# Routing ahead of the token split in a mixture-of-experts block: order of VectorE's work, layout of the tokens, and order of the first gather

## The chip, the cores and the metric

The kernel runs on one core of a Trainium2 chip. The metric is device time of one execution in microseconds (us), the median of several runs.

## The reference

One block of a diffusion transformer for 256 tokens of 1024 channels: modulation, input projections, four mixers (attention, a long convolution, two recurrences), a gated merge, and then a hierarchical mixture of experts. The change lies in the last:

```python
def _hier_moe(h, w_grp, b_grp, w_rt, b_rt, w1, w3, w2):
    t = h.reshape(-1, D_MODEL)
    gp = jax.nn.softmax((t @ w_grp + b_grp).astype(jnp.float32), axis=-1)
    g_val, g_idx = lax.top_k(gp, 1)                    # one of 4 groups
    el = (t @ w_rt + b_rt).astype(jnp.float32).reshape(-1, N_GROUPS, EXPERTS_PER_GROUP)
    el = jnp.take_along_axis(el, g_idx[:, :, None], axis=1)[:, 0]
    e_val, e_idx = lax.top_k(jax.nn.softmax(el, axis=-1), TOP_K_INNER)   # 2 of its 4 experts
    wts = g_val * e_val / jnp.sum(e_val, -1, keepdims=True)
    e_glob = g_idx * EXPERTS_PER_GROUP + e_idx
    combine = jnp.sum(jax.nn.one_hot(e_glob, N_EXPERTS, dtype=jnp.float32) * wts[..., None], axis=1)
    out = jnp.zeros_like(t)
    for e in range(N_EXPERTS):
        y = (jax.nn.silu(t @ w1[e]) * (t @ w3[e])) @ w2[e]
        out = out + combine[:, e:e + 1] * y
```

The block's result is `x + g2x * _hier_moe(_modulate(x, sh2x, sc2x), ...)`. Each expert has w1 and w3 of 1024x512 and w2 of 512x1024, all in float32.

## The kernel before, in words

Tokens lie on the 128 partitions in two halves (`a` = 0, 1). After the merge the kernel has `x2` (the tokens), `rx` (one over their root mean square) and the router's scores `lg`. From there:

- Choice. `rk` counts for each score how many of its four are larger; `og` is the chosen group, `sel` a 0/1 table of the two chosen experts, `oh` the first and second choice apart. `gm`, `ge`, `gv`, `so`, `w` are the weights (two exponentials, `ge` and `w`, run on ScalarE).
- Counting. Five small TensorE products of `sel` with ones and a triangle (`cntw`) give the tokens of each expert (`pn`, copied to `cntt`) and each token's place among its expert's (`pr`, copied to `pos`). `pm` is that place for the two static experts.
- Ranking. Experts 0 and 1 are static: 128 rows each. The other 14 are ranked by their count (`key`, `big`, `rank`, `roh`) and get rows in seven packed groups. `eidi` is the list of ranked experts; SyncE reads it into registers to address the weights of all later groups.
- Token split. `h2h` is the token times `rx` in the short float format of TensorE, `h2l` what rounding left. Half 0 of `h2l` is computed on VectorE, half 1 on GpSimd out of `sct`. ScalarE makes `h2h` and `sct`. Both tiles are laid out in 8 blocks of 128 channels, block j holding each eighth channel.
- Gather. `gather(gp)` brings the rows of two groups into `gT` by products with a 0/1 matrix `Dh` (256 columns): for each of the 8 blocks, two token halves, `h2h` and `h2l`, 32 products into PSUM tiles `mb`. The stationary side is a 128x128 block of `h2h` or `h2l`. ScalarE evicts the even blocks, VectorE the odd ones (`g<-mb,c`). There are five gathers.
- Experts. `expert_up` multiplies the gathered rows with w1 and w3 (PSUM tiles `hb`), `hidden` and `expert_down` follow, and a scatter by matrix product.

Weights come in 512 KB pieces on SyncE's queue into a ring of places (`wh`, `wwA`, `wB`, `wC`, `wD`, two of `g`); a place is free when TensorE has used its piece. The first 24 pieces belong to the static experts; later ones need `eidi`.

A scheduler sets the order of the instructions on each engine by what they depend on and by the order of the code; `after(x, y)` tells it to put x behind y, with no wait of its own. All operations go through one recording helper, so nearly every instruction of the profile has its line, L279; tile names tell them apart. L1550 is the read of `eidi` into a register. In a name such as `mb<-Dh,h2h` the tile after the comma is the stationary one.

Of the kernel before, what the change touches and what calls it, by code (L numbers as in the profile page):

```python
# [18 lines left out]
D = 1024  # L19
# [6 lines left out]
NSTAT = 2  # L26
# [260 lines left out]
def body(ctx, tc, I, out, dbg=None, upto=None):  # L287
    nc = tc.nc

    def after(ins, other):  # L290
        tc.add_manual_dep(ins.ins, other.ins.name, mybir.DependencyInfo(
            mybir.DependencyClass.NoSync, mybir.DependencyReason.SCHED_ONLY), reason="loads in order")
# [7 lines left out]
    def tap(name, ap):  # L300
        if name in dbg:
            nc.sync.dma_start(dbg[name], ap)
# [40 lines left out]
    def act(o, i, f=AF.Copy, **k):  # L343
        A.activation(out=o, in_=i, func=f, **k)

    def stt(o, a, s, b, op0=mul, op1=add, eng=V):
        return eng.scalar_tensor_tensor(out=o, in0=a, scalar=s, in1=b, op0=op0, op1=op1)

    def ts(o, a, s1, s2=None, op0=mul, op1=add, eng=V):
        if s2 is None:  # L350
            eng.tensor_scalar(out=o, in0=a, scalar1=s1, scalar2=None, op0=op0)
        else:
            eng.tensor_scalar(out=o, in0=a, scalar1=s1, scalar2=s2, op0=op0, op1=op1)

    def tt(o, a, b, op=mul, eng=V):
        eng.tensor_tensor(out=o, in0=a, in1=b, op=op)

    def cpy(o, i):
        return V.tensor_copy(out=o, in_=i)

    def red(o, i, op=add):
        return V.tensor_reduce(out=o, in_=i, axis=AX.X, op=op)
# [962 lines left out]
    def cl(name):  # L1325
        o, n = _CN[name]
        return late[:, o:o + n]
# [47 lines left out]
    def sm(name, shape, bufs=1, dt=F32):  # L1375
        return small(name, shape, bufs, p2, dt)
# [21 lines left out]
    ts(og, rk_[:, :, 0], 0.0, None, ALU.is_equal)  # L1398
    og4 = og.unsqueeze(3).to_broadcast([P, 2, 4, 4])
    sel = sm("sel", [2, 16], 1, F32R)  # L1400
    stt(sel.rearrange("p a (g e) -> p a g e", g=4), rk_[:, :, 1:5], 2.0, og4, ALU.is_lt, mul)

    pr, pn = mm(), mm()[:, :16]
    mmul(pn, cnt_w[:, 0], sel[:, 0], True, False)
# [1 line left out]
    mmul(pr[:, 0:16], cnt_w[:, 1], sel[:, 0])  # L1406
    mmul(pr[:, 16:32], cnt_w[:, 0], sel[:, 0], True, False)
    mmul(pr[:, 16:32], cnt_w[:, 1], sel[:, 1], False, True)

    nd = len(RANK)  # L1410
    key = sm("key", [nd])
    stt(key, pn[:, NSTAT:], 16.0, cl("rev"), mul, add)
    big3 = sm("big3", [nd, nd])
    rank = sm("rank", [nd])
    tt(big3, key.unsqueeze(1).to_broadcast([P, nd, nd]), key.unsqueeze(2).to_broadcast([P, nd, nd]), ALU.is_gt)
    ranked = red(rank, big3)
    roh = sm("roh", [nd, nd])
    tt(roh, rank.unsqueeze(1).to_broadcast([P, nd, nd]), cl("iota")[:, :nd].unsqueeze(2).to_broadcast([P, nd, nd]), ALU.is_equal)
    eidf, eidi = sm("eidf", [nd]), sm("eidi", [nd], 1, I32)
    big3 = sm("big3", [nd, nd])  # L1420
    tt(big3, roh, cl("eid").unsqueeze(1).to_broadcast([P, nd, nd]))
    red(eidf, big3)
    cpy(eidi, eidf)
    tap("eid", eidf)

    pos = sm("pos", [2, 16])
    after(cpy(pos, pr[:, 0:32].rearrange("p (a e) -> p a e", a=2)), ranked)
    pm = sm("pm", [2, NSTAT])
    stt(pm, pos[:, :, :NSTAT], 1.0, sel[:, :, :NSTAT].bitcast(F32), add, mul)

# [8 lines left out]
        return mb_("mb")  # L1439


    h2h, h2l = (slots.tile(p2, [P, 2, 8, 128], F32R, n, n, 1) for n in ("h2h", "h2l"))
    for a in range(2):
        xv = x2[:, a].rearrange("p (c j) -> p j c", j=8)
        act(h2h[:, a], xv, AF.Copy, scale=rx[:, a:a + 1])
        if a:
            for hf in range(2):
                t = slots.tile(p2, [P, 512], F32, "sct", "sct", 2)
                act(t, x2[:, a, hf * 512:hf * 512 + 512], AF.Copy, scale=rx[:, a:a + 1])
                hs = slice(hf * 64, hf * 64 + 64)  # L1450
                tt(h2l[:, a, :, hs], t.rearrange("p (c j) -> p j c", j=8), h2h[:, a, :, hs].bitcast(F32), sub, eng=G)
        else:
            stt(h2l[:, a], xv, rx[:, a:a + 1], h2h[:, a].bitcast(F32), mul, sub)


    cntt = sm("cntt", [16])
    cpy(cntt, pn)
    sb_, sc_ = sm("sb", [16]), sm("sc", [16])
    for dst, nm in ((sb_, "base"), (sc_, "cap")):
        cpy(dst[:, :NSTAT], cl("s" + nm))  # L1460
# [2 lines left out]
        red(dst[:, NSTAT:], big3)  # L1463
    oh = sm("oh", [2, 2, 16])
    for c in range(2):
        stt(oh[:, c].rearrange("p a (g e) -> p a g e", g=4), rk_[:, :, 1:5], float(c), og4, ALU.is_equal, mul)
    gm, ge, gv = sm("gm", [2, 1]), sm("ge", [2, 4]), sm("gv", [2, 1])
    red(gm, lg[:, :, 0:4], ALU.max)
    tt(ge, lg[:, :, 0:4], gm.to_broadcast([P, 2, 4]), sub)
    act(ge, ge, AF.Exp)  # L1470
    red(gv, ge)
# [88 lines left out]

    def gather(gp):

        Dh = slots.tile(p2, [P, 2, 256], F32R, "Dh", "Dh", 1)
        if gp == 0:
            for a in range(2):
                for e in range(2):
                    es = slice(e * 128, e * 128 + 128)
                    ts(Dh[:, a, es], cl("iota1"), pm[:, a, e:e + 1], None, ALU.is_equal)
            for a in range(2):
                for e in range(2):  # L1570
                    es = slice(e * 128, e * 128 + 128)
                    ts(Dw[:, a, es], cl("iota1"), pm[:, a, e:e + 1], we[:, a, e:e + 1], ALU.is_equal, mul)
        else:
            for a in range(2):
                ts(Dt[:, a], cl("iota"), sg[:, 0, a, gp:gp + 1], None, ALU.is_equal)
                stt(Dh[:, a], cl("iota"), sg[:, 1, a, gp:gp + 1], Dt[:, a], ALU.is_equal, add)
            for a in range(2):
                ts(Dt[:, a], Dt[:, a], w12[:, 0, a:a + 1])
                ts(Dw[:, a], cl("iota"), sg[:, 1, a, gp:gp + 1], w12[:, 1, a:a + 1], ALU.is_equal, mul)
                tt(Dw[:, a], Dw[:, a], Dt[:, a], add, eng=G)  # L1580
        for j2 in range(4):
            pg = mb()
            for jj in range(2):
                o = pg[:, jj * 256:jj * 256 + 256]
                j = 2 * j2 + jj
                for a in range(2):
                    mmul(o, h2h[:, a, j], Dh[:, a], a == 0, False)
                    mmul(o, h2l[:, a, j], Dh[:, a], False, a == 1)
                if jj:
                    ts(gT[:, j], o, c2[:, 1, j:j + 1], c2[:, 0, j:j + 1])  # L1590
                else:
                    act(gT[:, j], o, AF.Identity, scale=c2[:, 1, j:j + 1], bias=c2[:, 0, j:j + 1])

# [132 lines left out]
    with tc.If(over > 0):  # L1726
        slots.last.clear()
        cwl = sm("cwl", [2, 16])
        tt(cwl, we, lt_)
        for a in range(2):  # L1730
            hs_ = slots.tile(p2, [P, 8, 128], F32, "yeh", "yeh", 1)
            tt(hs_, h2h[:, a].bitcast(F32), h2l[:, a].bitcast(F32), add)
            for j4 in range(2):
                pt = mb()
                for jj in range(4):
                    j = 4 * j4 + jj
                    tr(pt[:, jj * 128:jj * 128 + 128], hs_[:, j])
                    act(gT[:, j, a * 128:a * 128 + 128], pt[:, jj * 128:jj * 128 + 128], AF.Identity,
                        scale=c2[:, 1, j:j + 1], bias=c2[:, 0, j:j + 1])
        for e in range(NE):  # L1740
            w13 = [[wload(name, e, q) for q in range(4)] for name in ("w1", "w3")]
            w2_ = [wload("w2", e, q) for q in range(4)]
            for a in range(2):
                as_ = slice(a * 128, a * 128 + 128)
                ph = []
                for ws in w13:
                    p = hb()
                    ph.append(p)
                    for j in range(8):
                        mmul(p, gT[:, j, as_], ws[j // 2][:, (j % 2) * 512:(j % 2) * 512 + 512], j == 0, j == 7)  # L1750
                a_ = slots.tile(p2, [P, 512], F32, "act", "act", 1)
                act(a_, ph[0], AF.Silu)
                tt(a_, a_, ph[1])
                pt = mb()
                for j in range(4):
                    tr(pt[:, j * 128:j * 128 + 128], a_[:, j::4])
                aT = slots.tile(p2, [P, 4, 128], F32, "aT", "aT", 1)
                act(aT.rearrange("p j s -> p (j s)"), pt)
                for hf in range(2):
                    hs = slice(hf * 512, hf * 512 + 512)  # L1760
                    po = mb()
                    for j in range(4):
                        mmul(po, aT[:, j], w2_[j][:, hs], j == 0, j == 3)
                    t = slots.tile(p2, [P, 512], F32, "sct", "sct", 2)
                    stt(t, po, cwl[:, a, e:e + 1], gg[0][:, 1, hs], mul, mul)
                    tt(x2[:, a, hs], x2[:, a, hs], t, add)
            places.extend(w13[0] + w13[1] + w2_)
        for a in range(2):
            SP.dma_start(ov[:, a], x2[:, a])
# [24 lines left out]
```

## Time and profile before

| | us |
|---|---|
| median of three runs | 779.45 |
| lowest and highest run | 777.98, 786.99 |
| profiled execution | 787.27 |
| its span in the trace | 785.5 |
| granted TensorE clock, mean share of full speed | 0.955 |
| TensorE busy | 720.7 (92%) |
| VectorE busy | 473.6 (60%) |
| ScalarE busy | 283.8 (36%) |
| GpSimd busy | 176.2 (22%) |

The span is the time from the first instruction to the last in the profiled execution; its own time is 1.8 us longer. The expert part takes the last third, from about 505 us. Starts in the rows below are us from the start of the span.

### The profile page before, as it was taken

The numbers are of one execution on the slowest core, as the hardware profiler recorded it, in microseconds if no ns is written. First come the engines' busy times: TensorE is split into PE (matmuls) and PEld (weight loads), VectorE is DVE, ScalarE is ACT, GpSimd is POOL, SyncE is SP. The second block draws the span as 40 slices with busy tenths as digits, with TensorE's granted clock in tenths as the row PEclk, the third lists the DMA queues.
The fourth block names the chain that finished last, engine by engine and source line by source line (L and its number), as shares of the span: only waits on it lengthen the run. The fifth ranks groups of instructions, "written<-read, shape, count | busy, mean of one in ns | idle before, by whom it ended". The sixth has DMA issues, their size and how long they took to land.

```text
span 785.5 us, 13522 instructions
## 1 busy us (share of the span) xinstructions
PE 720.7 (92%) x5155; PEld 503.6 (64%) x5155; DVE 473.6 (60%) x950; ACT 283.8 (36%) x530; POOL 176.2 (22%) x151
## 2 busy tenths in 40 slices
PE   3989998998889999999789998969999999999997
PEld 1658987887768667677689997754543434443334
DVE  5655467999993775899985377780422511432415
ACT  4333453533524676745346443440201102101111
POOL 0232232325421121122546474310000000000000
PEclk9979996999987999999989999969999999999999
DMA  8743220223332124668657688659799999999931
GB/s 321 246 182 108 86 76 28 55 82 109 111 105 55 29 81 162 195 213 288 202 207 269 220 298 308 240 168 410 274 376 409 408 408 409 409 409 410 388 99 57
DMA packets 53897, 174.97 MB, mean 223 GB/s; under 512 B 5442, under 2 KB 12482, under 8 KB 53826
## 3 DMA queue, kind: packets, MB, share of 16 engines
q1 hardware_dynamic: 50896, 168.79, 59.9%
q10 hardware_dynamic: 2930, 5.25, 2.0%
q8 instruction: 42, 0.69, 0.3%
q14 instruction: 29, 0.24, 0.1%
HBM read 172.97 MB, written 1.05 MB: 222 GB/s over the span
## 4 chain that ended last, share of the span: by engine, by line
PE 72%; DVE 20%; issue 3%; ACT 2%; POOL 1%; DMA 1%; SPq 0%; DVEq 0%; ACTq 0%; POOLq 0%
PE hb L279 26%; PE pj L279 18%; PE mm L279 14%; PE mo L279 9%; PE mb L279 7%; DVE wlo L279 3%; DVE TT L279 2%; DVE acc L279 2%; DVE tq L279 2%; DVE xt L279 1%; DVE L L279 1%; DVE gg L279 1%; DVE sin L279 1%; DVE hrc L279 1%; DMA hfp<-in_hfp_dram 1%
## 5 line engine op out<-in xcount | busy, mean ns | idle before, releaser
L279 PE MATMUL pj<-h,whi 128*128 128x256 f32 x1072 | 207.8, 293 | 4.7 <-DVE ylr L279 2.2
L279 PEld LDWEIGHTS pj<-h,whi 128*128 128x128 f32 x1072 | 172.6, 197 | 15.9 <-issue 9.3
L279 PE MATMUL pj<-h,wlo 128*128 128x256 f32 x536 | 158.8, 297 | 11.1 <-DVE wlo L279 10.5
L279 POOL TENSOR_TENSOR wlo<-raw,whi 128x512 fp32r<-128x512 f32 x64 | 90.0, 1405 | 196.2 <-ACT whi L279 176.4
L279 ACT ACTIVATE whi<-raw 128x512 fp32r<-128x512 f32 x130 | 81.1, 628 | 128.5 <-PE pj L279 105.9
L279 PEld LDWEIGHTS pj<-h,wlo 128*128 128x128 f32 x536 | 105.7, 197 | 15.9 <-DVE wlo L279 12.5
L279 DVE TENSOR_TENSOR wlo<-raw,whi 128x512 fp32r<-128x512 f32 x66 | 56.8, 861 | 23.3 <-ACT whi L279 23.0
L279 DVE TENSOR_TENSOR act<-act,hb 128x512 f32<-128x512 f32 x9 | 6.2, 688 | 96.7 <-PE hb L279 83.7
L279 PE MATMUL hb<-wwA,g 128*128 128x512 f32 (+2 forms) x200 | 59.8, 596 | 0.0
L279 POOL TENSOR_TENSOR gg<-gg 128x256 f32<-128x256 f32 x8 | 5.8, 741 | 183.0 <-DVE gg L279 183.0
L279 ACT ACTIVATE yeh<-sct,cw 128x512 fp32r<-128x512 f32 (+2 forms) x21 | 13.7, 661 | 76.1 <-DVE sct L279 75.6
L279 PEld LDWEIGHTS hb<-wwA,g 128*128 128x128 f32 (+2 forms) x200 | 20.8, 147 | 29.4 <-issue 27.2
L279 DVE TENSOR_TENSOR sct<-hb,gg 128x512 f32<-128x512 f32 (+2 forms) x21 | 12.8, 615 | 42.2 <-PE hb L279 42.2
L279 DVE SCALAR_TENSOR_TENSOR gg<-adaw,sT,gg 128x512 f32<-128x512 f32 x32 | 29.1, 931 | 2.4 <-ACT gg L279 2.3
L279 DVE TENSOR_TENSOR x<-mb,x 128x512 f32<-128x512 f32 (+2 forms) x42 | 23.7, 608 | 11.0 <-PE mb L279 11.0
L279 ACT ACTIVATE aT<-mb 128x512 f32<-128x512 f32 x9 | 5.4, 598 | 64.4 <-PE hb L279 33.4
L279 PE MATMUL mb<-Dh,h2h 128*128 128x256 f32 x80 | 24.1, 329 | 4.4 <-DVE eidi L279 3.7
L279 DVE SCALAR_TENSOR_TENSOR acc<-adaw,sT,acc 128x512 f32<-128x512 f32 x32 | 26.9, 874 | 0.0
L279 PE MATMUL hb<-wB,aT 128*32 128x512 f32 (+3 forms) x116 | 25.8, 508 | 0.0
L279 PE MATMUL hb<-wwA,aT 128*64 128x512 f32 (+2 forms) x96 | 24.1, 595 | 0.0
L279 PEld LDWEIGHTS mb<-Dh,h2h 128*128 128x128 f32 x80 | 16.8, 210 | 11.4 <-ACT g L279 4.1
L279 PE MATMUL hb<-wC,g 128*32 128x512 f32 (+2 forms) x88 | 23.4, 599 | 0.0
(482 smaller groups left out, 1455.0 us busy)
## 6 DMA issues: line engine op xcount, KB each, us to landing
wwA<-in_w_dram SPq DMA_DIRECT2D x72, 512.0 KB, 10.1
raw<-in_w_in_dram SPq DMA_DIRECT2D x57, 512.0 KB, 3.7
adaw<-in_ada_dram SPq DMA_DIRECT2D x48, 512.0 KB, 4.8
wB<-in_w_dram SPq DMA_DIRECT2D x35, 512.0 KB, 10.1
wC<-in_w_dram SPq DMA_DIRECT2D x24, 512.0 KB, 10.1
wh<-in_w_dram SPq DMA_DIRECT2D x22, 512.0 KB, 10.1
wD<-in_w_dram SPq DMA_DIRECT2D x17, 512.0 KB, 10.1
wb<-in_w_dram SPq DMA_DIRECT2D x10, 512.0 KB, 10.1
```

The source lines that it names most:

```text
L279: r = f(*a, **k)
```

## The change

The choice, the counts, the places and the first `Dh` (now `Dh0`) come ahead of VectorE's half of `h2l`, and this comes ahead of the ranking. First and second choice apart (`oh`), the largest group score (`gm`) and what follows from them come after the ranking. `key` reads the copy `cntt` and not PSUM. `h2h` and `h2l` keep the channels in their order, so that ScalarE, VectorE and GpSimd write and read them contiguously, and the products of all gathers read the stationary block with a stride of 8 elements (`j::8`). The first gather runs its 16 products with `h2h` before its 16 with `h2l`, into four PSUM tiles; VectorE's evictions of it stand behind the ranking.

```diff
-    stt(sel.rearrange("p a (g e) -> p a g e", g=4), rk_[:, :, 1:5], 2.0, og4, ALU.is_lt, mul)
+    selected = stt(sel.rearrange("p a (g e) -> p a g e", g=4), rk_[:, :, 1:5], 2.0, og4, ALU.is_lt, mul)
...
+    pos = sm("pos", [2, 16])
+    cpy(pos, pr[:, 0:32].rearrange("p (a e) -> p a e", a=2))
+    cntt = sm("cntt", [16])
+    cpy(cntt, pn)
+    pm = sm("pm", [2, NSTAT])
+    stt(pm, pos[:, :, :NSTAT], 1.0, sel[:, :, :NSTAT].bitcast(F32), add, mul)
...
+    h2h, h2l = (slots.tile(p2, [P, 2, D], F32R, n, n, 1) for n in ("h2h", "h2l"))
+    for a in range(2):
+        act(h2h[:, a], x2[:, a], AF.Copy, scale=rx[:, a:a + 1])
+    for hf in range(2):
+        t = slots.tile(p2, [P, 512], F32, "sct", "sct", 2)
+        hs = slice(hf * 512, hf * 512 + 512)
+        act(t, x2[:, 1, hs], AF.Copy, scale=rx[:, 1:2])
+        after(G.tensor_tensor(out=h2l[:, 1, hs], in0=t, in1=h2h[:, 1, hs].bitcast(F32), op=sub), selected)
+
+    Dh0 = slots.tile(p2, [P, 2, 256], F32R, "Dh", "Dh", 1)
+    for a in range(2):
+        for e in range(2):
+            es = slice(e * 128, e * 128 + 128)
+            last_dh = V.tensor_scalar(out=Dh0[:, a, es], in0=cl("iota1"), scalar1=pm[:, a, e:e + 1], scalar2=None,
+                                      op0=ALU.is_equal)
+    last_h2l = stt(h2l[:, 0], x2[:, 0], rx[:, 0:1], h2h[:, 0].bitcast(F32), mul, sub)
+    after(last_h2l, last_dh)
...
-    stt(key, pn[:, NSTAT:], 16.0, cl("rev"), mul, add)
+    after(stt(key, cntt[:, NSTAT:], 16.0, cl("rev"), mul, add), last_dh)
...
-    ranked = red(rank, big3)
+    red(rank, big3)
...
-    cpy(eidi, eidf)
+    ranked = cpy(eidi, eidf)
...
-    pos = sm("pos", [2, 16])
-    after(cpy(pos, pr[:, 0:32].rearrange("p (a e) -> p a e", a=2)), ranked)
...
-    h2h, h2l = (slots.tile(p2, [P, 2, 8, 128], F32R, n, n, 1) for n in ("h2h", "h2l"))
-    for a in range(2):
-        xv = x2[:, a].rearrange("p (c j) -> p j c", j=8)
-        act(h2h[:, a], xv, AF.Copy, scale=rx[:, a:a + 1])
...
-            stt(h2l[:, a], xv, rx[:, a:a + 1], h2h[:, a].bitcast(F32), mul, sub)
...
-        stt(oh[:, c].rearrange("p a (g e) -> p a g e", g=4), rk_[:, :, 1:5], float(c), og4, ALU.is_equal, mul)
+        after(stt(oh[:, c].rearrange("p a (g e) -> p a g e", g=4), rk_[:, :, 1:5], float(c), og4, ALU.is_equal, mul), ranked)
...
-    red(gm, lg[:, :, 0:4], ALU.max)
+    after(red(gm, lg[:, :, 0:4], ALU.max), ranked)
...
+        pgs = [mb() for _ in range(4)] if gp == 0 else [None] * 4
+
+        for j in range(8 if gp == 0 else 0):
+            for a in range(2):
+                mmul(pgs[j // 2][:, (j % 2) * 256:(j % 2) * 256 + 256], h2h[:, a, j::8], Dh[:, a], not (j % 2 or a), False, True)
...
-                    mmul(o, h2h[:, a, j], Dh[:, a], a == 0, False)
-                    mmul(o, h2l[:, a, j], Dh[:, a], False, a == 1)
+                    if gp:
+                        mmul(o, h2h[:, a, j::8], Dh[:, a], a == 0, False)
+                    mmul(o, h2l[:, a, j::8], Dh[:, a], False, a == 1, gp == 0)
...
-                    ts(gT[:, j], o, c2[:, 1, j:j + 1], c2[:, 0, j:j + 1])
+                    e_ = V.tensor_scalar(out=gT[:, j], in0=o, scalar1=c2[:, 1, j:j + 1], scalar2=c2[:, 0, j:j + 1],
+                                         op0=mul, op1=add)
+                    if not gp:
+                        after(e_, ranked)
```

How many instructions each engine has is the same before and after. On VectorE, between the token's scores and the first gather, this stood in a row before (`mm` is the PSUM tile of the counting products, `cstl` a table of constants):

```order
L279 SCALAR_TENSOR_TENSOR h2l<-x_4899,rx,h2h 128x1024
L279 TENSOR_SCALAR og<-rk 128x8
L279 SCALAR_TENSOR_TENSOR sel<-rk,og 128x32
L279 SCALAR_TENSOR_TENSOR oh<-rk,og 128x32 x2
L279 TENSOR_TENSOR so<-oh,lg 128x64
L279 SCALAR_TENSOR_TENSOR key<-mm,cstl 128x14
L279 COPY cntt<-mm 128x16
L279 TENSOR_TENSOR big_5540<-key 128x196
L279 TENSOR_REDUCE gv<-ge 128x2
L279 TENSOR_REDUCE w_5596<-so 128x4
L279 TENSOR_REDUCE rank<-big_5540 128x14
L279 COPY pos<-mm 128x32
```

There, now:

```order
L279 TENSOR_SCALAR og<-rk 128x8
L279 SCALAR_TENSOR_TENSOR sel<-rk,og 128x32
L279 COPY cntt<-mm 128x16
L279 COPY pos<-mm 128x32
L279 SCALAR_TENSOR_TENSOR pm<-pos,sel 128x4
L279 TENSOR_SCALAR Dh<-cstl,pm 128x128 x4
L279 SCALAR_TENSOR_TENSOR h2l<-x_4899,rx,h2h 128x1024
L279 SCALAR_TENSOR_TENSOR key<-cntt,cstl 128x14
L279 TENSOR_TENSOR big_5566<-key 128x196
L279 TENSOR_REDUCE rank<-big_5566 128x14
```

`h2l` has moved from ahead of the choice to behind the four `Dh`, and `pos` and `pm` from behind the ranking to ahead of it.

On TensorE, at the end of the first gather and the start of the static experts, before (`wh` and `wwA` are places of weights, `gg` the weighted one-hot that is transposed there):

```order
L279 MATMUL mb<-Dh,h2h 128x256
L279 MATMUL mb<-Dh,h2l 128x256
L279 MATMUL hb<-wh_5648,g_5633 128x512 x4
L279 MATMUL hb<-wwA,g_5633 128x512 x12
L279 MATMUL mb<-ident,gg 128x128 x2
```

The whole gather and this place, now:

```order
L279 MATMUL mm<-sel,cntw 128x16 x5
L279 MATMUL mb<-Dh,h2h 128x256 x16
L279 MATMUL mb<-Dh,h2l 128x256 x10
L279 MATMUL hb<-wh_5653,g_5638 128x512
L279 MATMUL mb<-Dh,h2l 128x256 x6
L279 MATMUL hb<-wwA,g_5638 128x512 x3
L279 MATMUL hb<-wh_5653,g_5638 128x512 x3
L279 MATMUL hb<-wwA,g_5638 128x512 x11
```

The alternating pairs have become 16 and 16, and four products that need block 0 of `gT` alone (one of `wh`, three of `wwA`) are drawn ahead of the products that need block 1.

On VectorE, around its evictions of the first gather, before:

```order
L279 TENSOR_REDUCE s_5613<-so 128x4
L279 TENSOR_SCALAR gg<-cstl,pm,we 128x128
L279 TENSOR_TENSOR sg<-s_5613,cstl 128x20
L279 TENSOR_SCALAR g_5633<-mb,c_112 128x256 x4
L279 TENSOR_SCALAR gg<-cstl,sg 128x256 x2
```

And now:

```order
L279 TENSOR_REDUCE gv<-ge 128x2
L279 TENSOR_TENSOR w_5601<-w_5601 128x2
L279 TENSOR_TENSOR late<-pos,sc 128x32
L279 RECIPROCAL gv<-gv 128x2
L279 TENSOR_TENSOR ovf<-cntt,sc 128x16
L279 SCALAR_TENSOR_TENSOR slot<-late,pos 128x32
L279 TENSOR_SCALAR w_5601<-w_5601 128x2
L279 TENSOR_REDUCE ovm<-ovf 128x1
L279 TENSOR_TENSOR slot<-slot,sb 128x32
L279 RECIPROCAL w_5601<-w_5601 128x2
L279 TENSOR_SCALAR ovm<-ovm 128x1
L279 TENSOR_SCALAR g_5638<-mb,c_112 128x256
```

The evictions stood behind all of the weights' arithmetic in one row; now they are spread through it, the first behind `gv` and two steps of `w`. On ScalarE the four evictions of the even blocks stood behind the exponentials `ge` and `w` and now stand ahead of them.

## Rows read from the trace of the kernel before

**Rows 1.** The page, chain that ended last: shares of the span by engine.

```profile
PE 72%; DVE 20%; issue 3%; ACT 2%; POOL 1%; DMA 1%; SPq 0%; DVEq 0%; ACTq 0%; POOLq 0%
```

**Rows 2.** Busy time by stretch, at the routing, the first gather and later.

```profile
core 0: us, PE busy (x) PEld busy (x) DVE busy (x) ACT busy (x) POOL busy (x), PEclk, DMA share, GB/s
515.00:520.00 5.00, 1.20 (x5) 1.14 (x5) 4.69 (x14) 2.97 (x4) 2.66 (x2) 0.50 0.12 48
526.00:527.00 1.00, 1.00 (x6) 1.00 (x6) 0.39 (x3) 0.98 (x3) 0.00 (x0) 0.50 0.94 242
527.00:528.00 1.00, 1.00 (x10) 1.00 (x9) 0.79 (x3) 0.82 (x1) 0.00 (x0) 0.94 0.87 291
555.00:575.00 20.00, 19.99 (x90) 10.09 (x88) 8.68 (x19) 3.51 (x6) 1.47 (x2) 1.00 0.72 246
700.00:720.00 20.00, 20.00 (x80) 7.62 (x78) 5.51 (x10) 3.68 (x6) 1.46 (x2) 1.00 1.03 409
```

**Rows 3.** Timeline of VectorE: start, length, tile and sources, and idle before.

```profile
514.65 2.06 DVE L279 SCALAR_TENSOR_TENSOR h2l<-x,rx,h2h 128x1024 fp32r<-128x1024 f32 x1
516.82 0.19 DVE L279 SCALAR_TENSOR_TENSOR sel<-rk,og 128x32 fp32r<-128x32 f32 x1
...
517.72 0.17 DVE L279 SCALAR_TENSOR_TENSOR key<-mm,cstl 128x14 f32<-128x14 f32 x1 [0.24 <-PE mm L279]
...
517.93 1.14 DVE L279 TENSOR_TENSOR big<-key 128x196 f32<-128x196 f32 x1
...
519.56 1.09 DVE L279 TENSOR_TENSOR roh<-rank,cstl 128x196 f32<-128x196 f32 x1
520.58 0.15 DVE L279 SCALAR_TENSOR_TENSOR pm<-pos,sel 128x4 f32<-128x4 f32 x1
...
520.73 0.34 DVE L279 TENSOR_TENSOR big<-roh,cstl 128x196 f32<-128x196 f32 x1
...
521.59 0.28 DVE L279 TENSOR_SCALAR Dh<-cstl,pm 128x128 fp32r<-128x128 f32 x1
521.78 0.16 DVE L279 CAST eidi<-eidf 128x14 int32<-128x14 f32 x1
```

**Rows 4.** Timeline of TensorE, from the counting products to the static experts' end.

```profile
517.12 1.20 PE L279 MATMUL mm<-sel,cntw 128*128 128x16 f32 x5 [4.01 <-issue]
522.01 0.55 PE L279 MATMUL mb<-Dh,h2h 128*128 128x256 f32 x1 [3.69 <-DVE eidi L279]
...
527.06 0.32 PE L279 MATMUL mb<-Dh,h2l 128*128 128x256 f32 x1
...
528.14 3.60 PE L279 MATMUL hb<-wh,g 128*128 128x512 f32 x8
...
556.30 0.38 PE L279 MATMUL mb<-ident,gg 128*128 128x128 f32 x2
```

**Rows 5.** Timeline of GpSimd.

```profile
517.34 3.10 POOL L279 TENSOR_TENSOR h2l<-sct,h2h 128x512 fp32r<-128x512 f32 x2 [7.15 <-ACT sct L279]
```

**Rows 6.** Waits of TensorE's weight loads, 528 to 745: total, times, longest.

```profile
PEld hb L279 <- DMA wwA<-in_w_dram: 2.0, 7, 0.4
```

**Rows 7.** Waits of SyncE's queue, 480 to 786.

```profile
SPq L279 <- PE hb L279: 42.7, 56, 5.4
```

**Rows 8.** Timeline of ScalarE.

```profile
512.48 4.17 ACT L279 ACTIVATE h2h<-x,rx 128x1024 fp32r<-128x1024 f32 x2 [1.99 <-DVE rx L279]
516.55 1.32 ACT L279 ACTIVATE sct<-x,rx 128x512 f32<-128x512 f32 x2
...
524.59 1.94 ACT L279 ACTIVATE g<-mb,c 128x256 f32<-128x256 f32 x4 [3.21 <-PE mb L279]
```

**Rows 9.** Groups of instructions by form, whole span: busy us, mean ns | idle before.

```profile
L279 ACT ACTIVATE wbh<-raw 128x1024 fp32r<-128x1024 f32 x6 | 6.3, 1058 | 11.3 <-PE mo L279 8.1 <-DVE wbl L279 2.4 <-DMA raw<-in_wb_dram 0.8
L279 PE MATMUL mo<-ident,x 128*128 128x128 f32 x8 | 1.2, 288 | 1.3 <-POOL x L279 1.3
L279 PE MATMUL mo<-ident,xin 128*128 128x128 f32 x32 | 4.7, 282 | 0.0
```

**Rows 10.** The same for GpSimd, 480 to 512.

```profile
L279 POOL TENSOR_TENSOR x<-x,gpw 128x512 f32<-128x512 f32 x2 | 2.5, 1278 | 3.7 <-DVE gpw L279 3.7
```

More of the change, by code (lines that the diff above doesn't have):

```diff
@@ L1408, in body @@
     mmul(pr[:, 16:32], cnt_w[:, 1], sel[:, 1], False, True)
-    nd = len(RANK)
-    key = sm("key", [nd])
-    stt(key, pn[:, NSTAT:], 16.0, cl("rev"), mul, add)
-    big3 = sm("big3", [nd, nd])
-    rank = sm("rank", [nd])
-    tt(big3, key.unsqueeze(1).to_broadcast([P, nd, nd]), key.unsqueeze(2).to_broadcast([P, nd, nd]), ALU.is_gt)
-    ranked = red(rank, big3)
[L1417 to L1422, printed above, removed]
-    cpy(eidi, eidf)
-    tap("eid", eidf)
     pos = sm("pos", [2, 16])
-    after(cpy(pos, pr[:, 0:32].rearrange("p (a e) -> p a e", a=2)), ranked)
+    cpy(pos, pr[:, 0:32].rearrange("p (a e) -> p a e", a=2))
+    cntt = sm("cntt", [16])
+    cpy(cntt, pn)
     pm = sm("pm", [2, NSTAT])
@@ L1439, in mb @@
         return mb_("mb")
-    h2h, h2l = (slots.tile(p2, [P, 2, 8, 128], F32R, n, n, 1) for n in ("h2h", "h2l"))
+    h2h, h2l = (slots.tile(p2, [P, 2, D], F32R, n, n, 1) for n in ("h2h", "h2l"))
     for a in range(2):
-        xv = x2[:, a].rearrange("p (c j) -> p j c", j=8)
-        act(h2h[:, a], xv, AF.Copy, scale=rx[:, a:a + 1])
[L1446 to L1452, printed above, removed]
-            stt(h2l[:, a], xv, rx[:, a:a + 1], h2h[:, a].bitcast(F32), mul, sub)
@@ L1456, in body @@
-    cntt = sm("cntt", [16])
-    cpy(cntt, pn)
+        act(h2h[:, a], x2[:, a], AF.Copy, scale=rx[:, a:a + 1])
[10 more added lines that the diff above has]
+                                      op0=ALU.is_equal)
@@ new lines, in body @@
+    last_h2l = stt(h2l[:, 0], x2[:, 0], rx[:, 0:1], h2h[:, 0].bitcast(F32), mul, sub)
+    after(last_h2l, last_dh)
+    nd = len(RANK)
+    key = sm("key", [nd])
+    after(stt(key, cntt[:, NSTAT:], 16.0, cl("rev"), mul, add), last_dh)
+    big3 = sm("big3", [nd, nd])
+    rank = sm("rank", [nd])
+    tt(big3, key.unsqueeze(1).to_broadcast([P, nd, nd]), key.unsqueeze(2).to_broadcast([P, nd, nd]), ALU.is_gt)
+    red(rank, big3)
+    roh = sm("roh", [nd, nd])
+    tt(roh, rank.unsqueeze(1).to_broadcast([P, nd, nd]), cl("iota")[:, :nd].unsqueeze(2).to_broadcast([P, nd, nd]), ALU.is_equal)
@@ L1458, in body @@
+    eidf, eidi = sm("eidf", [nd]), sm("eidi", [nd], 1, I32)
+    big3 = sm("big3", [nd, nd])
+    tt(big3, roh, cl("eid").unsqueeze(1).to_broadcast([P, nd, nd]))
+    red(eidf, big3)
+    ranked = cpy(eidi, eidf)
+    tap("eid", eidf)
     sb_, sc_ = sm("sb", [16]), sm("sc", [16])
@@ L1561, in gather @@
     def gather(gp):
-        Dh = slots.tile(p2, [P, 2, 256], F32R, "Dh", "Dh", 1)
+        Dh = Dh0 if gp == 0 else slots.tile(p2, [P, 2, 256], F32R, "Dh", "Dh", 1)
         if gp == 0:
-            for a in range(2):
-                for e in range(2):
-                    es = slice(e * 128, e * 128 + 128)
-                    ts(Dh[:, a, es], cl("iota1"), pm[:, a, e:e + 1], None, ALU.is_equal)
             for a in range(2):
@@ L1580, in gather @@
                 tt(Dw[:, a], Dw[:, a], Dt[:, a], add, eng=G)
+        pgs = [mb() for _ in range(4)] if gp == 0 else [None] * 4
+        for j in range(8 if gp == 0 else 0):
+            for a in range(2):
+                mmul(pgs[j // 2][:, (j % 2) * 256:(j % 2) * 256 + 256], h2h[:, a, j::8], Dh[:, a], not (j % 2 or a), False, True)
         for j2 in range(4):
-            pg = mb()
+            pg = pgs[j2] or mb()
             for jj in range(2):
@@ L1730, in body @@
         for a in range(2):
-            hs_ = slots.tile(p2, [P, 8, 128], F32, "yeh", "yeh", 1)
+            hs_ = slots.tile(p2, [P, D], F32, "yeh", "yeh", 1)
             tt(hs_, h2h[:, a].bitcast(F32), h2l[:, a].bitcast(F32), add)
@@ L1736, in body @@
                     j = 4 * j4 + jj
-                    tr(pt[:, jj * 128:jj * 128 + 128], hs_[:, j])
+                    tr(pt[:, jj * 128:jj * 128 + 128], hs_[:, j::8])
                     act(gT[:, j, a * 128:a * 128 + 128], pt[:, jj * 128:jj * 128 + 128], AF.Identity,
```

## The prediction

> **What bounds the kernel now.** I read the page first. The chain that ended last is TensorE (PE) for 72% and VectorE (DVE) for 20% [rows 1]: a TensorE kernel with a few stretches in which PE waits. So I looked for the stretch that the change touches, the start of the expert part, by windows. Between 515 and 520 us PE works 1.20 of 5 us, while DVE is busy for 4.69; from 555 on and still in 700 to 720 PE works all the time [rows 2]. The change is therefore worth what it takes out of the gap at 515 to 522, less what is given back behind it.
>
> DVE's timeline of that gap [rows 3] shows one engine doing things in a row. Before the choice `sel` it spends 2.06 us on `h2l`, which nobody needs yet; `sel` is done at 517.01. The five counting products run on PE from 517.12 to 518.32 [rows 4]. Then DVE ranks experts: `big` 1.14, `roh` 1.09 us, although the second `big`, of the same 128x196 size, takes 0.34. The first two lie on the two `h2l` instructions of GpSimd (POOL), which run from 517.34 to 520.44 [rows 5]: some 0.8 and 0.75 us are a wait for it. `pm` ends at 520.73, the second half of `Dh` at 521.87, and the first gather product starts at 522.01 [rows 4]. `eidi`, on which the later weight loads hang, ends at 521.94.
>
> Behind the gather PE is the bound. Its 32 products take 522.01 to 528.14, and the rows show why so long: in 526 to 527 the granted clock is still 0.50 of full speed (the 1.2 GHz level), in 527 to 528 it is 0.94 [rows 2]. The 23 products before 527.06 take 0.22 us each, the nine from there 0.12 [rows 4]. The up products of the two static experts end at 556.30. For weights PE waits little: the largest entry is 2.0 us in 7 waits of at most 0.4 [rows 6]. But DMA is near its limit too: 409 GB/s in 700 to 720. In 555 to 575 it moves 246 GB/s, which by that rate leaves (1 - 246/409) x 20 = 8.0 us of slack [rows 2]; there the queue waits for PE to free places, as it does 56 times, for 42.7 us [rows 7]. So if PE comes earlier by less than 8 us, the transfers can come earlier with it.
>
> **The change part by part.** (1) `h2l` leaves the way of `sel`: -2.06 us. `sel` ends at about 514.95 and the five products at 516.3.
>
> (2) `cntt`, `pos` and `pm` come next (0.17 each for the copies, as for `key`, a small read of PSUM too, the first while PE still counts, and 0.15 [rows 3]), so `pm` is issued at about 516.45. Before, the first key stood at 517.72 and `pm` ended at 520.73: ranking and its waits lay between. That goes off the path.
>
> (3) Whether POOL holds `pm` up. ScalarE's `h2h` reads and writes with a stride now and takes 2.09 each (4.17 for two); the contiguous 128x1024 copy `wbh` takes 1.06 [rows 8, 9]. So `h2h` ends at 514.6 instead of 516.65, `sct` at 515.3 and 515.9, and POOL starts at 515.3 with 1.28 each (a contiguous 128x512 operation [rows 10]): 516.6 and 517.9. `pm` reads two SBUF tiles, as `big` and `roh` do, which waited. In the trace `big` got its turn between POOL's two instructions (3.10 = 2 x 1.38 + 0.34). If `pm` does too, it ends at 516.75; if it comes just after POOL's second began, at 518.0. Two `Dh` of 0.28 follow, and 0.14 to the first product as now: G, the start of the gather, is at 517.45 or at 518.75, against 522.01. That is -4.6 or -3.3. I take the first, since `pm` is reckoned at 516.45 and the boundary at 516.6, and shade it to -4.4 because that margin is thin.
>
> (4) The gather from G on: as many products, the clock as before (5.1 us of low clock after the start, then full). `h2l` of DVE starts after the fourth `Dh`, near 518.2, and is done by 520.3 even at its old 2.06; POOL's is done by 517.9. The first product that needs either is the seventeenth, at G + 3.5 = 521. No stall: 0.
>
> (5) Evictions to `gT`. ScalarE's four (1.94 us [rows 8]) end at about G + 6.2; the exponentials `ge` and `w` stand behind them now. DVE's four stand behind the whole ranking, and behind `gv`, which needs `ge`. DVE: ranking from 520.3, without POOL's holds 4.2 - 1.55 = 2.65 us, so `eidi` ends near 522.9 at worst (521.94 now); some twenty small instructions and the two passes to ScalarE, and the first eviction starts at about G + 8.5. PE meanwhile has the gather to G + 6.1 and four products on `gT` block 0 that are drawn forward, 0.88 each (28.2 us for 32, 528.14 to 556.30 [rows 4], with what little lies between): it asks for block 1 at G + 9.6. One microsecond of margin: 0 on the path, and -1 to +3 if I am off by that much.
>
> (6) `eidi` at 521.2 to 522.9 instead of 521.94: the loads that hang on it wait for places that PE frees later: 0.
>
> (7) Layout. Tokens are kept in channel order, so the stationary side of all 160 gather products is read with a stride of 8 elements (32 bytes). Nearest row: the transposes `mo` of `x`, whose stationary tile is read with the same stride, take 1.2 us for eight, 150 ns each at most; those of `xin`, contiguous, 4.7 / 32 = 147 [rows 9]. So 0, and at most the 6 ns by which their means differ (288, 282), 160 x 6 = 1.0 us. I take +0.4.
>
> Against that stands the first half of the same comparison on another engine: ScalarE took twice as long for a strided copy. The Trainium skill, page "SBUF — State Buffer", section "Door 1: The DMA port swizzle", says that SBUF serves 16-byte lines, that full speed needs two hits in a line, and that four fp32 elements is as far as a free stride goes; this change puts one element in each line for PE's loads. By that rule the sum would be that of rival B below; the trace agrees where ScalarE is concerned, 2.09 against 1.06 us, and disagrees where PE is, 150 against 147 ns.
>
> Sum: -4.4 + 0 + 0 + 0.4 = -4.0. The profiled execution, 787.27 (span 785.5 and 1.8 around it), would become 783.3. It stands 7.8 above the median of the runs, 779.45, which is in the same difference **775.5 us**.
>
> **Rivals.**
> D, more: PE's clock rises sooner in the gather, since its products follow the counting products after 1.2 us and not 3.7. 23 products at 0.12 instead of 0.22 give 2.3 us more: up to -6.3, 773.2.
>
> C, the evictions late: if DVE reaches block 1 at 3 us past the reckoning, PE stands 2 us: 777.5. The same time comes out if `pm` is held and the clock rises at 527.1 whatever PE does (then about 2.7 us of up products run at half speed, and 1.3 is lost). For it: DVE's queue is in order and waits twice on ScalarE there. Against: the four products drawn forward cover it.
>
> A, given back: weights come at 409 GB/s to the end, and PE catches up with them. For it: the waits on `wwA` exist already. Against: 8.0 us of slack at 555. It leaves 0.5: 778.9.
>
> B, slower: the strided stationary read. If a load takes twice as long, as ScalarE's copy does, a gather product at full clock goes from 0.12 to 0.24; the 128 of gathers 1 to 4 run at full clock, +15; the first gather's, at half clock, have room. With -4.0 it gives +11, 790.5. It decides from 4.0 / 128 = 31 ns per load upward. For it: the ScalarE row. Against: the transposes, the same engine and stride.
>
> **How the numbers follow.** Forecast (773.9 to 777) 0.54, D 0.12, C 0.14, A 0.14, B 0.06. The likeliest is 775.5. The range 771.8 to 781.5 holds all but B, with the two ends that far out because the runs of before lie apart by more than the gain. Two per cent, 15.6 us, is about what a measurement of this kernel tells from no change; only B at its worst comes near it. Faster 0.02, same 0.95, slower 0.03.
>
> **What would show it.** In the trace after: `sel` ended 0.3 us behind `rk`; `pm` issued 1.5 us later and shorter than 0.6 (or above 1: held); the first gather product 4.9 to 6.2 us after `h2h` starts (9.5 now); `h2h` at 1.06 each; 16 products with `h2h` then 16 with `h2l`, in 6.1 us or, for D, clearly less. No gap on PE before block 1 (C). The end of both up products at the same distance from G, 34.3. Gather products at 0.12 in gathers 1 to 4 (B: over 0.15). PE's waits for `wwA`, `wB`, `wD` not above 6 us in sum (A). I am wrong if the gather starts early and the end of the kernel does not move, or if the gather products spread.

## The result: slower, and the profile after

The changed kernel takes 803.54 us in the median of four runs, against 782.32 for the kernel before in its four: ratio 1.027, 95% interval 1.020 to 1.034. The profiled execution took 806.62 us, its span 804.8. Forecast were 775.5 and a range up to 781.5; the sign is wrong too.

The page of the kernel after first. The chain that ended last answers to [rows 1]: TensorE's share has risen from 72 to 75%.

```profile
PE 75%; DVE 17%; issue 2%; ACT 2%; POOL 1%; DMA 1%; SPq 0%; DVEq 0%; POOLq 0%; ACTq 0%
```

The start of the expert part went about as forecast. VectorE's timeline of the kernel after, which answers to [rows 3]:

```profile
517.72 0.19 DVE L279 SCALAR_TENSOR_TENSOR sel<-rk,og 128x32 fp32r<-128x32 f32 x1
518.61 0.17 DVE L279 COPY cntt<-mm 128x16 f32<-128x16 f32 x1 [0.70 <-PE mm L279]
519.25 0.19 DVE L279 COPY pos<-mm 128x32 f32<-128x32 f32 x1 [0.46 <-PE mm L279]
519.48 1.21 DVE L279 SCALAR_TENSOR_TENSOR pm<-pos,sel 128x4 f32<-128x4 f32 x1
520.72 0.87 DVE L279 TENSOR_SCALAR Dh<-cstl,pm 128x128 fp32r<-128x128 f32 x4
521.51 1.28 DVE L279 SCALAR_TENSOR_TENSOR h2l<-x,rx,h2h 128x1024 fp32r<-128x1024 f32 x1
```

ScalarE and GpSimd beside it (two views of the kernel after; [rows 5, 8] before):

```profile
515.30 2.19 ACT L279 ACTIVATE h2h<-x,rx 128x1024 fp32r<-128x1024 f32 x2 [1.98 <-DVE rx L279]
...
518.18 2.48 POOL L279 TENSOR_TENSOR h2l<-sct,h2h 128x512 fp32r<-128x512 f32 x2 [5.16 <-ACT sct L279]
```

`h2h` takes 2.19 for both, about as reckoned (4.17 before). `pm` took 1.21 us in place of 0.15: it was issued at 519.48, when GpSimd's second `h2l` had just begun, and ended when that did, at 520.66. This is the later of the two values given in the prediction.

TensorE's timeline of the kernel after, which answers to [rows 4], from the first gather to the second:

```profile
518.01 1.20 PE L279 MATMUL mm<-sel,cntw 128*128 128x16 f32 x5 [2.08 <-issue]
521.35 4.10 PE L279 MATMUL mb<-Dh,h2h 128*128 128x256 f32 x16 [2.13 <-DVE Dh L279]
525.28 2.58 PE L279 MATMUL mb<-Dh,h2l 128*128 128x256 f32 x10
527.70 1.02 PE L279 MATMUL hb<-wh,g 128*128 128x512 f32 x2
528.16 1.89 PE L279 MATMUL mb<-Dh,h2l 128*128 128x256 f32 x6
529.88 2.74 PE L279 MATMUL hb<-wwA,g 128*128 128x512 f32 x6
...
557.19 0.38 PE L279 MATMUL mb<-ident,gg 128*128 128x128 f32 x2
557.33 0.49 PE L279 MATMUL mb<-Dh,h2h 128*128 128x256 f32 x1
557.65 0.41 PE L279 MATMUL mb<-Dh,h2l 128*128 128x256 f32 x1
557.89 0.40 PE L279 MATMUL mb<-Dh,h2h 128*128 128x256 f32 x1
558.13 0.40 PE L279 MATMUL mb<-Dh,h2l 128*128 128x256 f32 x1
```

Look at the starts in the last rows: 557.65, 557.89, 558.13. Products of the second gather, at full clock, start 0.24 us apart where a product took 0.12 [rows 4]. That alone is 15 us in the 128 products of gathers 2 to 5 (which the prediction numbers 1 to 4).

Programs begin this part at different times even where they are equal up to there: `h2h` starts between 508.8 and 522.0 in the eight profiles of the table, before any edit takes effect. So I compare distances from the start of `h2h` on, read from the timelines. G is the first gather product; "2nd" and "5th" are the first products of those gathers; "end" is the end of the span. The columns e1 to e7 are the experiments below; e5, whose edit lies ahead of this stretch, is not among them.

```
us                  before  after   e1     e2     e3     e4     e6     e7
start of h2h to G     9.53   6.05   5.00   9.25   5.01   6.25   5.00   5.00
G to 2nd gather      34.43  35.98  35.67  36.15  35.44  35.81  35.69  34.91
2nd to 5th gather   150.42 164.93 153.70 161.26 153.82 164.23 152.20 153.07
5th gather to end    78.64  82.58  78.67  82.52  78.76  82.34  78.49  78.61
sum                 273.02 289.54 273.04 289.18 273.03 288.63 271.38 271.59
```

The kernel after is 16.5 us longer in this stretch: -3.5 to G, then +1.6, +14.5 and +3.9. Its whole span is 19.3 longer; 2.8 of that is the later start of `h2h`, in a part that the change does not touch. The medians differ by 21.2; what lies between that and 16.5 is not explained here, and runs of the kernel before alone lie 9 us apart. The profile of e6 is of a slow execution (795.12 us); only its distances are used, and its granted clock from the second gather to 785 us is 1.00, as in e1.

### The profile page after: what moved, and what is told of

Read it like the earlier page. It is cut to its first block, busy times and chain, and to the rows that moved or that the text cites. A ratio compares the mean times of both kernels' runs of the same rounds, so it can differ in the third digit from the quotient of the medians.

```text
span 804.8 us, 13517 instructions
## 1 busy us (share of the span) xinstructions
PE 740.5 (92%) x5155; PEld 520.6 (65%) x5155; DVE 470.0 (58%) x950; ACT 282.3 (35%) x530; POOL 179.0 (22%) x151
## 4 chain that ended last, share of the span: by engine, by line
PE 75%; DVE 17%; issue 2%; ACT 2%; POOL 1%; DMA 1%; SPq 0%; DVEq 0%; POOLq 0%; ACTq 0%
PE hb L279 25%; PE pj L279 18%; PE mm L279 13%; PE mo L279 10%; PE mb L279 9%; DVE TT L279 2%; DVE wlo L279 2%; DVE tq L279 2%; DVE acc L279 2%; DVE xt L279 1%; DVE L L279 1%; POOL s L279 1%; DVE sin L279 1%; DMA hfp<-in_hfp_dram 0%; ACT whi L279 0%
## 5 line engine op out<-in xcount | busy, mean ns | idle before, releaser
L279 DVE TENSOR_TENSOR wlo<-raw,whi 128x512 fp32r<-128x512 f32 x66 | 54.3, 824 | 26.7 <-ACT whi L279 26.7
L279 PE MATMUL mb<-Dh,h2h 128*128 128x256 f32 x80 | 32.0, 437 | 2.9 <-DVE Dh L279 2.1
L279 PEld LDWEIGHTS mb<-Dh,h2h 128*128 128x128 f32 x80 | 25.2, 333 | 11.3 <-issue 5.2
L279 PE MATMUL mb<-Dh,h2l 128*128 128x256 f32 x80 | 30.5, 410 | 0.0
L279 ACT ACTIVATE g<-mb,c 128x256 f32<-128x256 f32 x20 | 11.0, 565 | 48.1 <-PE mb L279 22.9
L279 PEld LDWEIGHTS mb<-Dh,h2l 128*128 128x128 f32 x80 | 25.7, 336 | 2.2 <-issue 1.6
```

What stands on the lines that cost most here:

```text
L279: r = f(*a, **k)
```

## The experiments

Theory S: the strided read of the gather's stationary blocks costs all of it. Rival T: the new order of work costs it. The first two kernels each do one half of the change.

**e1, the order alone.** The changed kernel with block layout and contiguous loads:

```diff
-        act(h2h[:, a], x2[:, a], AF.Copy, scale=rx[:, a:a + 1])
+        act(lay(h2h[:, a]), chan(x2[:, a]), AF.Copy, scale=rx[:, a:a + 1])
...
-                    mmul(o, h2l[:, a, j::8], Dh[:, a], False, a == 1, gp == 0)
+                    mmul(o, blk(h2l, a, j), Dh[:, a], False, a == 1, gp == 0)
```

`lay` and `chan` arrange the tile and the token in 8 blocks of 128 channels; `blk` takes one block.

> The changed kernel with its order of work on every engine kept, but h2h and h2l laid out in blocks of 128 channels as before, so that the gather's stationary blocks are read contiguously again. Theory S (the strided stationary read costs all of it): gather products 0.12 us apart at full clock in gathers 1 to 4, against 0.24 in the changed kernel; the first gather product comes 5 to 6.2 us after rx (9.6 before, 6.1 changed), and the kernel is 3 to 5 us faster than before, ratio 0.994 to 0.997. Rival T (the order costs: two passes of the gather, evictions behind the ranking, work of later groups in another order): gather products 0.12 apart all the same, but the kernel is slower than before by 5 us or more, ratio above 1.006.

Measured: ratio to before 1.0036, interval 0.998 to 1.009. The gather products are 0.12 apart; TensorE's timeline of e1, second gather:

```profile
555.73 0.28 PE L279 MATMUL mb<-Dh,h2l 128*128 128x256 f32 x1
555.85 0.28 PE L279 MATMUL mb<-Dh,h2h 128*128 128x256 f32 x1
555.97 0.28 PE L279 MATMUL mb<-Dh,h2l 128*128 128x256 f32 x1
```

G comes 5.00 us after `h2h` starts, 4.5 earlier than before. `h2h` reads the token with a stride again and takes 4.21 us, so GpSimd starts only when `pm` is done; it then runs beside `Dh` and `h2l`. VectorE's and GpSimd's timelines of e1, then TensorE's of the first gather:

```profile
519.03 0.16 DVE L279 SCALAR_TENSOR_TENSOR pm<-pos,sel 128x4 f32<-128x4 f32 x1
519.23 2.14 DVE L279 TENSOR_SCALAR Dh<-cstl,pm 128x128 fp32r<-128x128 f32 x4
...
519.75 3.02 POOL L279 TENSOR_TENSOR h2l<-sct,h2h 128x512 fp32r<-128x512 f32 x2 [7.19 <-ACT sct L279]
```

```profile
521.51 2.90 PE L279 MATMUL mb<-Dh,h2h 128*128 128x256 f32 x12 [0.46 <-DVE Dh L279]
524.64 2.04 PE L279 MATMUL mb<-Dh,h2l 128*128 128x256 f32 x10 [0.23 <-DVE h2l L279]
```

But the sum of the stretch is 273.04, to 0.02 that of before. So S holds for the loss, and both S and T missed the rest: the order's 4.5 us are all given back, 1.2 up to the second gather and 3.3 between the second and the fifth. Half of the latter is one wait in TensorE's timeline of e1, where the scatter of a group stands right behind the group's own w2 products:

```profile
620.25 1.94 PE L279 MATMUL hb<-wwA,aT 128*64 128x512 f32 x8
623.76 0.73 PE L279 MATMUL mb<-yeh,DT 128*128 128x512 f32 x2 [1.57 <-ACT yeh L279]
624.43 1.06 PE L279 MATMUL hb<-wwA,g 128*32 128x512 f32 x6
```

The kernel after has the same wait, at 633.01 with the same 1.57 us. In the kernel before, six up products of a 32-row group and the transposes stand between the w2 products and the scatter, and TensorE has no wait there:

```profile
619.45 1.06 PE L279 MATMUL hb<-wwA,g 128*32 128x512 f32 x6
620.44 0.75 PE L279 MATMUL mb<-ident,act 128*128 128x128 f32 x4
...
621.16 0.47 PE L279 MATMUL mb<-yeh,DT 128*128 128x512 f32 x1
```

**e2, the layout alone.** The kernel before, its order untouched, with channel order and strided loads:

```diff
-        xv = x2[:, a].rearrange("p (c j) -> p j c", j=8)
+        xv = x2[:, a]
...
-                    mmul(o, h2h[:, a, j], Dh[:, a], a == 0, False)
+                    mmul(o, h2h[:, a, j::8], Dh[:, a], a == 0, False)
```

> The kernel before with one edit: h2h and h2l keep the channels in their order, written contiguously, and the gather reads its stationary blocks with a stride of 8 elements. Order of the work as before. Theory S: gather products 0.24 us apart in all five gathers; 128 x 0.12 = 15 us in gathers 1 to 4 and 1 to 2 in the first, less up to 1 from the shorter h2h: ratio 1.018 to 1.025. Rival T: less than 5 us, ratio below 1.006.

Measured: ratio 1.017, interval 1.012 to 1.023, just below the 1.018 to 1.025 of S; the stretch is 16.2 us longer than before, of the 16.5 of the whole change. TensorE's timeline of e2, second gather:

```profile
555.68 0.40 PE L279 MATMUL mb<-Dh,h2l 128*128 128x256 f32 x1
555.92 0.40 PE L279 MATMUL mb<-Dh,h2h 128*128 128x256 f32 x1
556.16 0.41 PE L279 MATMUL mb<-Dh,h2l 128*128 128x256 f32 x1
```

The products are 0.24 apart. The layout is the loss; the order, by e1, is worth nothing on balance.

**e3 and e4, a stride of 2 and of 4.** The changed kernel with `LS = 2` and `LS = 4` in

```python
    def blk(t, a, j):
        o = (j // LS) * 128 * LS
        return t[:, a, o + j % LS:o + 128 * LS:LS]
```

and the tiles written to match, in two instructions where there was one.

> The changed kernel with a layout in which a stationary block is read with a stride of 2 elements (8 bytes) in place of 8 (32 bytes); the tiles are written in two instructions each. If the price hangs on how many elements share 16 bytes (two here), gather products are 0.12 us apart. If any stride costs, 0.24.

> The same with a stride of 4 elements (16 bytes), one element in each 16 bytes. If the price hangs on elements that share 16 bytes, gather products are 0.24 us apart, as with stride 8. If a stride of up to 4 elements is free, 0.12.

TensorE's timeline of e3, second gather, then that of e4:

```profile
554.53 0.28 PE L279 MATMUL mb<-Dh,h2l 128*128 128x256 f32 x1
554.65 0.28 PE L279 MATMUL mb<-Dh,h2h 128*128 128x256 f32 x1
554.77 0.29 PE L279 MATMUL mb<-Dh,h2l 128*128 128x256 f32 x1
```

```profile
551.15 0.40 PE L279 MATMUL mb<-Dh,h2l 128*128 128x256 f32 x1
551.38 0.40 PE L279 MATMUL mb<-Dh,h2h 128*128 128x256 f32 x1
551.62 0.40 PE L279 MATMUL mb<-Dh,h2l 128*128 128x256 f32 x1
```

One execution each took 788.75 and 799.18 us, beside a median of 790.17 for before on that chip. A stride of 2 elements (8 bytes) is free, 0.12; at a stride of 4 (16 bytes) products are 0.23 to 0.24 apart, nearly as with 8. So the edge lies above 8 bytes and at 16 at the latest; a count of two elements in each 16 bytes fits, and so would a limit on the step itself, since a stride of 3 was not run. The Trainium skill, page "SBUF — State Buffer", section "Door 1: The DMA port swizzle", says that a 16-byte line needs two hits for full speed; the trace agrees for these loads, 0.12 with two and 0.23 with one. The same place gives a stride of four fp32 elements as free; e4, at 0.23 against 0.12, does not bear that out.

**e5, why the transposes misled.** The prediction had taken its price from transposes with the same stride. Here the second half of them is made as plain float32 products with the identity, four contiguous ones (overwritten) and then the four strided ones, and this twice:

```diff
-                tr(pt[:, jj * 128:jj * 128 + 128], x2[:, a, 4 * j4 + jj::8])
+                if not a:
+                    tr(pt[:, jj * 128:jj * 128 + 128], x2[:, a, 4 * j4 + jj::8])
+            for jj in range(4 if a else 0):
+                j = 4 * j4 + jj
+                mmul(pt[:, jj * 128:jj * 128 + 128], x2[:, a, j * 128:j * 128 + 128], ident)
+            for jj in range(4 if a else 0):
+                mmul(pt[:, jj * 128:jj * 128 + 128], x2[:, a, 4 * j4 + jj::8], ident)
```

> The kernel before, with the second half of the transposes of x (the eight into pj) made as plain float32 products with the identity: in each group of four, first four with contiguous stationary blocks (their result is written over), then the four with stride 8 that are wanted. Theory S2: the strided read costs a plain product's load twice its time, and the transposes, which stood in the prediction as evidence, read that operand in another way: the strided plain products are about twice as far apart as the contiguous ones just ahead of them, while the transposes of the first half stay at 0.11 us. Rival: a stride costs nothing in float32, and only the gather's format (fp32r) pays for it: contiguous and strided plain products are equally far apart.

Busy time by stretch of e5 (length, then each engine's busy time with its instructions in parentheses): eight strided transposes, eight contiguous instructions (a float32 product is two), eight strided ones, and the last two again:

```profile
508.60:509.50 0.90, 0.90 (x8) 0.90 (x9) 0.90 (x2) 0.87 (x3) 0.00 (x0) 1.00 1.03 419
509.60:510.40 0.80, 0.80 (x9) 0.80 (x9) 0.80 (x3) 0.77 (x3) 0.00 (x0) 1.00 0.58 236
510.50:512.30 1.80, 1.80 (x9) 1.80 (x9) 1.61 (x10) 0.25 (x2) 0.54 (x2) 1.00 0.23 50
512.40:513.20 0.80, 0.80 (x9) 0.80 (x9) 0.66 (x5) 0.60 (x1) 0.00 (x0) 1.00 0.72 205
513.30:514.80 1.50, 1.50 (x8) 1.50 (x8) 0.28 (x2) 0.00 (x0) 0.00 (x0) 1.00 0.93 309
```

Nine instructions lie in 0.80 us where the block is contiguous, and nine need 1.80 where it is strided; from start to start it is 0.11 and 0.24. The strided transposes pass at 0.11. So the price is not one of the gather's number format, and it does not apply to a transpose that reads the same tile with the same stride. It is also the same for a product of 128 columns here and of 256 in the gather. What a transpose does otherwise with that operand the rows do not show.

**e6, the wait in the middle covered.** e1 with one rule of order more, for group 2:

```diff
+            m_ = mmul(po, DT[rows, as_], yh[rows, cs], True, False)
+            if cover_[0] is not None:
+                after(m_, cover_[0])
...
+            cover_[0] = ups_.get(g + 2) if g in (2,) else None
```

`ups_[g]` is the last of group g's first four blocks of w1 products.

> The changed order with block layout (as in the order alone), and one rule of order more: the scatter of group 2 stands behind the first four w1 products of group 4, so that TensorE has work while ScalarE makes yeh. Theory G (the 4.5 us that the order wins at the start are given back, 2 us of them in TensorE's wait for yeh in the middle of the expert part): that wait of 1.57 us is gone, and the stretch from rx to the end is 1.5 to 2.5 us shorter than with the order alone: 271 us, against 273.1 in both kernels so far; ratio 0.996 to 1.0. Rival: something else fills its place (the weight stream), and the stretch stays at 273.

Measured: ratio 0.997, interval 0.992 to 1.001, no difference that this shows; the stretch from `h2h` is 271.38, 1.66 shorter than e1's and 1.64 shorter than before. TensorE's timeline of e6 at this place:

```profile
627.39 1.94 PE L279 MATMUL hb<-wwA,aT 128*64 128x512 f32 x8
629.26 1.92 PE L279 MATMUL hb<-wwA,g 128*32 128x512 f32 x16
631.00 1.90 PE L279 MATMUL hb<-wC,g 128*32 128x512 f32 x16
632.83 0.50 PE L279 MATMUL mb<-yeh,DT 128*128 128x512 f32 x1
```

The wait is gone, and its time is won: theory G holds for this part, in one profile. The 1.8 us that remain against before between the second and the fifth gather are not one wait but spread, 1.0 of it over the starts of products of 32-row groups; I did not follow them further.

**e7, GpSimd out of the stretch.** e6, with both halves of `h2l` on VectorE and `sct` left out:

```diff
-        act(t, x2[:, 1, hs], AF.Copy, scale=rx[:, 1:2])
...
+    for a in range(2):
+        last_h2l = stt(lay(h2l[:, a]), chan(x2[:, a]), rx[:, a:a + 1], lay(h2h[:, a]).bitcast(F32), mul, sub)
+        after(last_h2l, last_dh)
...
-    after(stt(key, cntt[:, NSTAT:], 16.0, cl("rev"), mul, add), last_dh)
+    after(stt(key, cntt[:, NSTAT:], 16.0, cl("rev"), mul, add), last_h2l)
```

> The same as the run before, with GpSimd's half of h2l moved to VectorE (two instructions of one kind in place of one, and sct left out), so that nothing on GpSimd can hold VectorE in this stretch. If GpSimd's share cost the first gather its 1.3 us (Dh 2.14 for four, h2l 3.30), then Dh takes 0.9 for four, h2l 2.1 each, the second pair of Dh no longer delays the gather, and the gather waits about 1 us for the second h2l instead: within 0.5 us of the run before. If VectorE is the bound there, the evictions of the first gather come late and TensorE waits 1 to 2 us more.

Measured: ratio 1.000, interval 0.996 to 1.004; stretch 271.59. VectorE's timeline of e6, with GpSimd at work from 526.83 to 529.89, and then that of e7:

```profile
526.33 2.15 DVE L279 TENSOR_SCALAR Dh<-cstl,pm 128x128 fp32r<-128x128 f32 x4
528.40 3.32 DVE L279 SCALAR_TENSOR_TENSOR h2l<-x,rx,h2h 128x1024 fp32r<-128x1024 f32 x1
```

```profile
518.80 0.87 DVE L279 TENSOR_SCALAR Dh<-cstl,pm 128x128 fp32r<-128x128 f32 x4
519.60 4.20 DVE L279 SCALAR_TENSOR_TENSOR h2l<-x,rx,h2h 128x1024 fp32r<-128x1024 f32 x2
```

Without GpSimd the four `Dh` take 0.87 in place of 2.15, and an `h2l` 2.1 in place of 3.32. So GpSimd's work was the hold. The edit wins 0.8 us up to the second gather (34.91 against 35.69); between the second and the fifth, where the order of products differs, 0.9 is lost again. In the 0.8 a sooner clock has a part that these runs do not separate: the granted clock is 0.66 from 523 to 524 us in e7, some 4 us after G, and still 0.50 from 532 to 533 us in e6, 5 to 6 us after G.

## Why the prediction was wrong

**The step that failed is (7), the layout.** It took +0.4, at most 1.0 us, from the transposes of `x`, the nearest row with the same engine and the same stride. A transpose and a product do not pay alike for a strided stationary operand: 0.11 and 0.24 us on the same tile (e5), and the 160 gather products paid the second price. Rival B named the mechanism and its place, doubled loads in gathers 1 to 4, and its +15 us agree with the 16.2 of e2, where the first gather adds 1.7 (36.15 against 34.43). I gave it 0.06, since I let the nearest-looking row outweigh ScalarE's, whose copy at half speed with the same stride was the better witness, and the rule of the Trainium skill that the prediction quotes. B's +11 fell short of the 16.5 of the stretch: the start gave -3.5, near its -4.0, but it had nothing for the first gather (+1.6) and nothing for the order of later products (3.3).

**Steps (1) to (3), the start: right.** -3.5 of the two values -4.6 and -3.3; the one that was called less likely came, with `pm` held by GpSimd as described. In e1 and e7 nothing holds `pm`, and G is 4.5 earlier. One reading in (3) was wrong without changing the sum: `h2h` of the kernel before is written contiguously, block after block, and only the token is read with a stride, so ScalarE's 2.09 against 1.06 us is the price of a strided read, as TensorE's is.

**Step (4), the first gather: right on the stall, wrong on the pace and the clock.** TensorE does not wait in it: `h2l` is done at 522.79, and its first product stands at 525.28. But its strided products are 0.24 apart at either level of the clock. And the clock rose some 3.4 us after G, not 5.1 as before (0.63 is the mean of a microsecond that begins at 0.50 and ends at 1.00):

```profile
524.00:525.00 1.00, 1.00 (x6) 1.00 (x6) 0.90 (x5) 0.00 (x0) 0.00 (x0) 0.63 0.00 0
```

That is rival D's condition in part; its gain could not come while the products stayed 0.24 apart. With contiguous blocks (e1) there is a stall, 0.46 us for `Dh` and 0.23 for `h2l`, and 1.2 us are lost up to the second gather. With GpSimd gone (e7) 0.8 of that comes back, so most of it hangs on GpSimd's hold on `Dh` and on `h2l`, by the waits and by the later clock; I had reckoned that hold for `pm` only.

**Step (5), evictions: right.** VectorE's first eviction starts at 528.99, 7.6 after G (8.5 reckoned), and TensorE goes on to the up products without a wait. Rival C did not occur.

**The sum left out the order of later products.** The scheduler puts the middle of the expert part in another order when the start is edited, though nothing there was touched, and one scatter lost its cover: 1.6 us (e1, e6). The prediction has no term for it and gives no reason for leaving it out. Rival A gave the right time for the order alone, no gain, for a wrong reason: the weights do not account for it, since TensorE's weight loads wait 0.8 us for `wwA` and `wD` in e1 and 1.8 before (519 to 645 us). The wait for `yeh` does for half of the 3.3; of the rest about half lies in the products of 32-row groups, and why these take longer stays open.

Of the 16.5 us: -3.5 at the start, +1.6 up to the second gather, +15.1 from strided loads in gathers 2 to 5 (the kernel after against e1) and +3.3 from the later order (e1 against before). In the 1.6 the shares do not add up singly: the layout alone costs 1.7 there (e2) and the order alone 1.2 (e1). No version here beats the kernel before by more than the measurement can tell; e6 comes nearest.

## What to carry to other kernels

Lay out a tile for whoever reads it most often: the strided read of the token costs ScalarE 1 us for each half of `h2h`, once, while a strided stationary block costs TensorE 0.12 us at each of 128 loads at full clock. When a price is taken from a neighbouring row, ask whether the instruction is of the same kind, and not only of the same engine and access; here a transpose said nothing of a product. And where a scheduler orders the work, compare the whole order, also far from the edit: a gain at the start can be lost at a place that the diff never names.

## What was not expected of the hardware

- A stationary block read with at most one float32 element in each 16 bytes makes products 0.24 us apart (0.23 at a stride of 4), with two elements in 16 bytes 0.12, as contiguous. At a stride of 8 this pace does not follow TensorE's clock. Busy time by stretch of the kernel after, first gather at the 1.2 GHz level and at the 2.4 GHz level (the number behind GpSimd's is the granted clock):

```profile
522.00:523.00 1.00, 1.00 (x6) 1.00 (x6) 0.97 (x3) 0.00 (x0) 0.00 (x0) 0.50 0.00 0
525.00:526.00 1.00, 1.00 (x5) 1.00 (x6) 1.00 (x7) 0.00 (x0) 0.00 (x0) 1.00 0.00 0
```

  Six and five instructions touch a microsecond at either level; before, the products were 0.22 and 0.12 apart [rows 4].
- Transposes of blocks with the same stride pass at 0.11 us (e5).
- GpSimd holds VectorE's `Dh` too, which has one tile and a column of scalars as inputs: 2.15 against 0.87 us for four (e6, e7).
